# First norm by diagonal products, first stretch in a written order: one change to a hybrid streaming block on Trainium2

## The chip, the cores and the metric

The kernel runs on one core of a Trainium2 chip. A core has five engines that take their instructions from queues of their own and wait for each other by semaphores: TensorE (PE, matrix products, with PEld for its weight loads), VectorE (DVE), ScalarE (ACT), GpSimd (POOL) and SyncE (SP, which here only issues DMAs). The metric is the device time of one execution in microseconds (us), shown as a median of several runs. One execution of each kernel is also recorded by the hardware profiler; its span runs from the first instruction to the last.

## What is computed

The reference is one layer of an encoder over 1024 tokens of 1024 channels, all in float32. Cut to what matters here:

```python
def rmsnorm(x, g):
    y = x * lax.rsqrt(jnp.mean(x * x, axis=-1, keepdims=True) + EPS)
    return y * g

def swiglu(x, w_gate, w_up, w_down):
    return (jax.nn.silu(x @ w_gate) * (x @ w_up)) @ w_down

def reference(x, ...):
    x = x + 0.5 * swiglu(rmsnorm(x, ffn1_norm[l]), ffn1_w_gate[l], ffn1_w_up[l], ffn1_w_down[l])
    h = rmsnorm(x, mix_norm[l])
    ...
    x = x + 0.5 * swiglu(rmsnorm(x, ffn2_norm[l]), ffn2_w_gate[l], ffn2_w_up[l], ffn2_w_down[l])
    return rmsnorm(x, final_norm)
```

The inner width of each SwiGLU is 2816. The change concerns the first line: the first norm, and the first products that use it.

## The kernel before

**Precision.** Each float32 operand of a large product is split into a high part (a cast to fp32r on ScalarE) and a low part (the remainder, on VectorE or GpSimd). A product is three matmuls, high times high, high times low and low times high (`mm3`, all recorded at line 53). `split` makes both parts of a weight (L61, L62).

**Chunks.** The 2816 inner channels are 22 chunks of 128. Chunks 1 to 21 make gate and up together by a scheme of seven products instead of eight over 2 x 2 blocks (`gu`, 84 matmuls of 512 columns each). The normed, transposed x stands in four blocks: B11 (tokens of tiles 0 to 3, channels 0 to 511), B12 (tiles 4 to 7, channels 0 to 511), B21 (tiles 0 to 3, channels 512 to 1023), B22 (tiles 4 to 7, channels 512 to 1023). To these come four sums of blocks, T1 to T4, and sums of weight blocks, `s` (GpSimd, L191, in `load_gu`), whose split parts are named `gs`.

**The first stage.** Chunk 0 does not need the sums: `gu_plain` makes it by the eight plain products, in two halves of 256 columns per block, the first from token tiles 0, 1, 4 and 5, the second from 2, 3, 6 and 7: 96 matmuls a half. So TensorE has 64 transposes of 128 x 128, 192 matmuls of 256 columns and then chunk 1's 84 of 512 to do up to chunk 2. Chunk 1's products need T sums and split weight sums.

The norm comes ahead of the transposes. `normed` takes one tile of 128 tokens: square with a sum on ScalarE (L74), mean on VectorE (L76), the power on GpSimd (L70), and x times the factor times the norm row on VectorE (L82, a full row `grow` of 1024 values on each partition). The second four tiles have the same at L488 to L493. `blocks` then transposes by a product with the identity (L95) into a bank of PSUM, and ScalarE and VectorE take it out: the high and low parts of each block (`put`, L118 and L119; B12's at L141, L142) and the differences t3, t1, t2, t4 (L133, L137, L148, L150). `put_sums` makes the T sums from these, the T3 difference on GpSimd (L157).

**What sets the order.** The code is written loop by loop; a scheduler then reorders the built instructions of each engine by its own costs, and pools decide when a tile may be reused. Transfers of one queue (SP's and ScalarE's) are issued in the order in which the scheduler leaves them. Behind chunk 0, `weight_sums` makes sums of the down weights (loads L285, GpSimd L278, stores L293), for chunk pairs, and `hidden_sums` stores the hidden values (L296 to L307). PSUM has eight banks here, four under the tag "mm" for results, four under "ax".

## Time and profile before

| | |
|---|---|
| median of 3 runs | 1850.05 us (1845.16 to 1851.8) |
| the profiled execution's own time | 1841.2 us |
| its span | 1839.4 us |
| TensorE busy | 97% of the span |
| mean TensorE clock granted | 0.992 |

The profile gives the busy time of each engine, groups of instructions by line, and the timeline of each engine. In a timeline row stand the start and length in us, engine, line, operation, what it writes and reads, shape and count, and in brackets the idle time before it with what ended it. In a row of a stretch stand the busy times of PE, PEld, DVE, ACT and POOL, each with its count, then the granted clock of TensorE (1.00 is full), the mean busy share of the DMA engines and the GB/s moved. A wait of an engine that is not the bottleneck costs nothing by itself.

### The profile page before, as it was taken

The page shows a single profiled execution, that of the slowest core. Times are in us where ns is not written, and L with a number is a line of the kernel's source. Part 1 is how long each engine was busy: PE and PEld are TensorE (multiplying, and loading weights), DVE is VectorE, ACT ScalarE, POOL GpSimd, SP SyncE. Part 2 cuts the span into 40 slices and gives each one's busy share as a digit, 9 for nine tenths or more (in the row PEclk, how much of TensorE's full clock was granted, in tenths as well). Part 3 has the DMA queues.
Part 4 walks back from the last instruction along what each step waited for, and adds up shares of the span by engine and source line. Part 5 has one row for each costly group of instructions (what it writes and reads, how often), then busy time and mean ns, then how long its engine had stood idle before and what let it go on. Part 6 is the DMA issues. An engine that isn't in the chain of part 4 may idle for free.

```text
span 1839.4 us, 25484 instructions
## 1 busy us (share of the span) xinstructions
PE 1784.1 (97%) x9735; PEld 1524.8 (83%) x9735; DVE 1191.7 (65%) x1531; ACT 686.6 (37%) x1193; POOL 747.9 (41%) x583
## 2 busy tenths in 40 slices
PE   5999999999999999898999999999999999999997
PEld 4888888888788889797788989988888888878886
DVE  6867676665565575769655344587776766656546
ACT  6333332333343454432344533452333323243433
POOL 4667666565140012212132420366666665614001
PEclk9999999999999999999999999999999999999999
DMA  5353443544957445453432254334535445495744
GB/s 196 108 175 136 162 152 134 184 158 163 339 188 258 155 177 164 140 195 100 133 94 67 90 197 136 109 104 165 178 132 171 144 154 188 142 344 185 264 142 149
DMA packets 134441, 302.26 MB, mean 164 GB/s; under 512 B 27408, under 2 KB 42032, under 8 KB 134320
## 3 DMA queue, kind: packets, MB, share of 16 engines
q1 hardware_dynamic: 131824, 296.20, 46.9%
q10 hardware_dynamic: 2496, 4.44, 0.8%
q8 instruction: 76, 1.25, 0.3%
q14 instruction: 45, 0.37, 0.1%
HBM read 208.83 MB, written 91.77 MB: 163 GB/s over the span
## 4 chain that ended last, share of the span: by engine, by line
PE 78%; DVE 8%; DMA 5%; POOL 4%; issue 3%; ACT 2%; SPq 0%; POOLq 0%; DVEq 0%; ACTq 0%
PE mm L53 43%; PE ax L53 32%; POOL s L191 1%; POOL t L278 1%; DMA left<-hq 1%; DVE acc L873 1%; PE ax L95 1%; PE sd L53 1%; DMA graw<-in_f1gu_dram 1%; POOL s L278 1%; PE sc L53 1%; DVE T L119 0%; DVE unit L62 0%; DVE wk L62 0%; DVE E L797 0%
## 5 line engine op out<-in xcount | busy, mean ns | idle before, releaser
L53 PE MATMUL mm<-unit 128*128 128x512 f32 x1056 | 244.9, 392 | 4.2 <-ACT unit L61 2.2
L53 PEld LDWEIGHTS mm<-unit 128*128 128x128 f32 x1056 | 198.8, 189 | 47.4 <-ACT unit L61 3.3
L191 POOL TENSOR_TENSOR s<-graw 128x512 f32<-128x512 f32 x84 | 130.3, 1551 | 262.9 <-DMA graw<-in_f2gu_dram 116.0
L62 DVE TENSOR_TENSOR ga<-graw,ga 128x512 fp32r<-128x512 f32 x134 | 155.9, 1166 | 99.9 <-ACT ga L61 99.2
L61 ACT CAST gs<-s 128x512 fp32r<-128x512 f32 x168 | 104.5, 622 | 301.8 <-PE mm L53 151.0
L62 DVE TENSOR_TENSOR unit<-left,unit 128x1024 fp32r<-128x1024 f32 x84 | 101.9, 1215 | 133.0 <-ACT unit L61 132.3
L53 PE MATMUL ax<-T,gs 128*128 128x512 f32 x792 | 183.1, 389 | 0.0
L53 PE MATMUL ax<-unit 128*128 128x512 f32 x792 | 180.5, 389 | 0.0
L53 PEld LDWEIGHTS ax<-T,gs 128*128 128x128 f32 x792 | 148.7, 188 | 30.8
L53 PEld LDWEIGHTS ax<-unit 128*128 128x128 f32 x792 | 148.7, 188 | 30.8
L62 DVE TENSOR_TENSOR gs<-s,gs 128x512 fp32r<-128x512 f32 x168 | 172.7, 1030 | 2.3
L53 PE MATMUL mm<-B,ga 128*128 128x512 f32 (+1 forms) x864 | 166.8, 347 | 3.3 <-ACT B L118 1.9
L61 ACT CAST unit<-left 128x1024 fp32r<-128x1024 f32 x84 | 82.5, 982 | 230.2 <-PE ax L53 100.5
L53 PE MATMUL mm<-T,gs 128*128 128x512 f32 x720 | 166.5, 389 | 0.0
L53 PEld LDWEIGHTS mm<-B,ga 128*128 128x128 f32 x864 | 139.5, 194 | 23.4 <-ACT B L118 2.5
L53 PEld LDWEIGHTS mm<-T,gs 128*128 128x128 f32 x720 | 135.2, 188 | 28.0
L70 POOL TENSOR_TENSOR rs<-rs,half 128x1 f32<-128x1 f32 (+1 forms) x29 | 19.2, 662 | 334.5 <-DVE rs L76 334.4
L53 PE MATMUL mm<-actT,wk 128*128 128x512 f32 x576 | 150.4, 403 | 0.0
L53 PE MATMUL ax<-B,ga 128*128 128x512 f32 x528 | 127.2, 390 | 1.4 <-DVE ga L62 1.4
L53 PE MATMUL mm<-wk,actT 128*128 128x256 f32 x960 | 123.5, 285 | 2.7 <-DVE wk L62 2.7
L53 PEld LDWEIGHTS mm<-wk,actT 128*128 128x128 f32 x960 | 117.4, 190 | 3.4 <-DVE wk L62 3.0
L53 PEld LDWEIGHTS mm<-actT,wk 128*128 128x128 f32 x576 | 103.6, 188 | 18.8
(239 smaller groups left out, 3046.0 us busy)
## 6 DMA issues: line engine op xcount, KB each, us to landing
left<-hq SPq DMA_DIRECT2D x70, 512.0 KB, 5.0
graw<-in_f1gu_dram SPq DMA_DIRECT2D x44, 512.0 KB, 5.4
wq<-t SPq DMA_DIRECT2D x44, 512.0 KB, 2.8
hq<-s SPq DMA_DIRECT2D x44, 512.0 KB, 3.1
graw<-in_f2gu_dram SPq DMA_DIRECT2D x44, 512.0 KB, 4.7
right<-wq SPq DMA_DIRECT2D x40, 512.0 KB, 4.8
wd<-in_f1wd_dram SPq DMA_DIRECT2D x22, 512.0 KB, 6.6
hq<-sg SPq DMA_DIRECT2D x22, 512.0 KB, 3.7
```

Source lines behind the costliest of these rows:

```text
L53: nc.tensor.matmul(*args, **kw)
L61: nc.scalar.copy(h, src)
L62: nc.vector.tensor_tensor(l, src, h, op=ALU.subtract)
L70: nc.gpsimd.tensor_tensor(o, i, half[:, :w], op=ALU.pow)
L95: nc.tensor.transpose(ps[:, i * P:(i + 1) * P], blk(i), ident)
L191: nc.gpsimd.tensor_tensor(f, u, v, op=op)
L278: nc.gpsimd.tensor_tensor(o, u, v, op=op)
L873: nc.vector.scalar_tensor_tensor(acc, pad[:, j:j + 512], cw[:, blk, j:j + 1], acc, op0=ALU.mult, op1=ALU.add)
```

## The change

The first norm is no longer made on x. ScalarE squares a tile, GpSimd adds the constant and takes the power, and ScalarE multiplies the identity by the four factors of a group of tiles: a 128 x 128 diagonal per tile (`factors`, L545 and L550 of the changed kernel). TensorE multiplies x's columns by that diagonal, which transposes and scales at once (`turn` in `scaled_blocks`), where before it transposed: 64 float32 products of 128 x 128 in place of 64 transposes. The norm's gain, which now lies along partitions, is a factor in each evacuation: `put` and `t3` on ScalarE (L166, L188: a multiplication), `less` on VectorE (L163: multiply and subtract). It comes as a small load of 128 x 8 values (`f1g`) in place of the full row.

A column of `scaled_blocks` is one bank: 128 channels by 512 tokens, u (the tiles of B11 or B21) and v (those of B12 or B22). For columns 0 to 3, ScalarE makes B11's high part, t3 and B12's high part and VectorE B11's low part, B12's low part and t1; for columns 4 to 7, ScalarE makes the high parts of B21 and B22 and VectorE both low parts, t2 and t4.

Further: x is loaded in the order 0, 1, 4, 5, then 2, 3, 6, 7; 20 products of the identity with itself stand ahead of all others on TensorE, and are used by nothing; the table of Silu is loaded at the start; `gu_plain` yields in groups of 12 products and goes through the channels one after the other in this stage; each T sum's parts are made for 256 columns at once (`scaled_sum`); the order on TensorE, VectorE, ScalarE and GpSimd up to the last T part and weight split of chunk 1 is the one in which the code is written (`manual_schedule`); the down-weight sums of the first pair go from chunk 1 to chunk 2; the loads of norm rows keep their place in the written order. Four working tiles of the second half come from the pools of x (three) and of raw weights (`t4`, under the tag "graw"). The second SwiGLU computes as before, with the changed function called through `together`.

```diff
-        nc.scalar.dma_start(g, a[name].to_broadcast([P, D]))
+        tc.keep_in_program_order(nc.scalar.dma_start(g, a[name].to_broadcast([P, D])))
...
-        def put(self, n, i, src, eng):
+        def __init__(self, qp, bp):
+            self.qp, self.bp, self.B, self.f = qp, bp, {}, {}
+        def block(self, n):
             if n not in self.B:
                 if n in ("T1", "T3", "B21"):
                     self.B[n] = act_tile(self.bp, "cmb", n, bufs=3)
                 else:
                     self.B[n] = act_tile(name=n)
-            t = self.B[n][:, :, :, i * P:i * P + P]
+            return self.B[n]
+        def put(self, n, i, src, eng):
+            t = self.block(n)[:, :, :, i * P:i * P + P]
             nc.scalar.copy(t[:, 0], src)
             eng.tensor_tensor(t[:, 1], src, t[:, 0], op=ALU.subtract)
 
...
+        def scaled_blocks(self, i, pp, xts, dg, g, f, b12, ahead):
+            sl = slice(i * 256, i * 256 + 256)
+            t3, t1, t2, t4 = self.f[i] = f
+            def less(o, src, c, v):
+                nc.vector.scalar_tensor_tensor(o, src, g[:, c:c + 1], v, op0=ALU.mult, op1=ALU.subtract)
+            def put(h, l, src, c):
+                nc.scalar.mul(h, src, g[:, c:c + 1])
+                less(l, src, c, h)
+            banks = []
+            def turn(k):
+                cs = range(len(banks), len(banks) + k)
+                banks.extend(bank(*pp) for _ in cs)
+                for n, x in enumerate(xts):
+                    for c in cs:
+                        mm(banks[c][:, n * P:n * P + P], x[:, c * P:c * P + P], dg[:, n * P:n * P + P], start=True, stop=True)
+            turn(ahead)
+            for c in range(8):
+                if c == len(banks):
+                    turn(1)
+                u, v = banks[c][:, :256], banks[c][:, 256:]
+                k = c % 4
+                if c < 4:
+                    b = self.block("B11")
+                    put(b[:, 0, k, sl], b[:, 1, k, sl], u, c)
+                    nc.scalar.mul(t3[:, k], u, g[:, c:c + 1])
+                    b = b12[k // 2]
+                    put(b[:, 0, k % 2], b[:, 1, k % 2], v, c)
+                    less(t1[:, k], v, c, t3[:, k])
+                else:
+                    b = self.block("B21")
+                    put(b[:, 0, k, sl], b[:, 1, k, sl], u, c)
+                    b = self.block("B22")
+                    put(b[:, 0, k, sl], b[:, 1, k, sl], v, c)
+                    less(t2[:, k], v, c, t1[:, k])
+                    less(t4[:, k], u, c, t2[:, k])
+                yield
+        def scaled_diff(self, i):
+            t3, _, t2, _ = self.f[i]
+            nc.gpsimd.tensor_tensor(t3, t2, t3, op=ALU.subtract)
+        def scaled_sum(self, i, n, eng):
+            src = self.f[i][{"T1": 1, "T2": 2, "T3": 0, "T4": 3}[n]]
+            t = self.block(n)[:, :, :, i * 256:i * 256 + 256]
+            nc.scalar.copy(t[:, 0], src)
+            eng.tensor_tensor(t[:, 1], src, t[:, 0], op=ALU.subtract)
...
-        def gu_plain(sl, b12):
+        def gu_plain(sl, b12, by_k=False):
             g = gu_s[0]
             w = sl.stop - sl.start
             gates, ups = ([bank(*A)[:, :w] for _ in range(2)] for _ in range(2))
             xs = {n: partial(lambda n, s, k, sl: B[n][:, s, k, sl], n) for n in ("B11", "B21", "B22")}
             xs["B12"] = lambda s, k, sl: b12[k // 2][:, s, k % 2]
-            for i, x in ((0, "B11"), (1, "B12"), (0, "B21"), (1, "B22")):
-                first = x[1] == "1"
-                for p, wt in ((gates[i], g["B11" if first else "a12"]), (ups[i], g["a21" if first else "a22"])):
-                    products(p, wt, xs[x], sl, first, not first)
+            todo = [(first, k, i, j) for first in (True, False) for k in range(4) for i in range(2) for j in range(2)]
+            if not by_k:
+                todo.sort(key=lambda s: (not s[0], s[2], s[3], s[1]))
+            for n, (first, k, i, j) in enumerate(todo):
+                x = xs[(("B21", "B22"), ("B11", "B12"))[first][i]]
+                p, wt = (gates[i], ups[i])[j], g[(("a12", "a22"), ("B11", "a21"))[first][j]]
+                mm3(p, wt[:, 0, k], wt[:, 1, k], x(0, k, sl), x(1, k, sl), first and k == 0, not first and k == 3, skip_group_check=True)
+                if n % 4 == 3:
+                    yield
 ...
         start(SimpleNamespace(load_gu=load_gu, gu=gu, gu_plain=gu_plain, gtile=gtile, A=A, X=X))
         xts = {}
         for c in range(1, NCH):
-            together(load_gu(c))
-            if c % 2:
+            if c not in gu_s:
+                together(load_gu(c))
+            if c % 2 and c > late:
                 weight_sums(c // 2)
-            else:
+            elif c % 2 == 0:
+                if c // 2 * 2 == late + 1:
+                    weight_sums(0)
                 hidden_sums(c // 2 - 1)
...
-    xs = load_x(xdram, (0, 4))
-    g = grow("ffn1_norm")
-    xs.update(load_x(xdram, (1, 5)))
+    nc.scalar.dma_start(g1, a["f1g"])
+    xs = load_x(xdram, (0, 1, 4, 5))
...
-            def xi(i):
-                return xs[i], xs[i + 4]
-            uv = [cb.sums() for _ in range(2)]
-            for j in range(2):
-                for i in range(2):
-                    normed(xi(i)[j], g, xi(i)[j], uv[i][j])
+            order = ((0, 1, 4, 5), (2, 3, 6, 7))
+            def factors(ts):
+                ms, rs = (sm.tile([P, 4], F32, tag=n, name=n) for n in ("ssk", "rk"))
+                dg = rp.tile([P, 544], F32, tag="sf", name="dg", bufs=4)[:, :512]
+                for n, t in enumerate(ts):
+                    junk = f.gtile(F32, "junk").rearrange("p s n -> p (s n)")
+                    m, r = ms[:, n:n + 1], rs[:, n:n + 1]
+                    nc.scalar.activation(junk, xs[t], AF.Square, scale=D ** -0.5, accum_out=m)
+                    nc.gpsimd.tensor_scalar(r, m, EPS, None, op0=ALU.add)
+                    rpow(r, r, 1)
+                yield dg
+                for n in range(4):
+                    nc.scalar.mul(dg[:, n * P:n * P + P], ident, rs[:, n:n + 1])
+                yield
...
+            def four(ts):
+                return [t.rearrange("p a (b n) -> p (a b) n", b=2) for t in ts]
+            E = mybir.EngineType
-            together(*(cb.put_sums(i, ("T2", "T1", "T3", "T4"), (V, G, V, G)) for i in range(4)))
+            with tc.manual_schedule(engines={E.PE, E.DVE, E.Activation, E.Pool}):
+                warm = bank(*f.X)
+                for _ in range(20):
+                    mm(warm[:, :P], ident, ident, start=True, stop=True)
+                nc.scalar.activation(half[:, 7:8], half[:, 6:7], AF.Silu)
+                facs = [factors(t) for t in order]
+                dg = next(facs[0])
+                together(facs[0])
+                together(f.load_gu(0, True))
+                xs.update(load_x(xdram, order[1]))
+                b = b12()
+                bl = cb.scaled_blocks(0, f.X, [xs[t] for t in order[0]], dg, g1, four(cb.sums() + cb.sums()), b, 4)
+                pr = f.gu_plain(slice(0, 256), b, True)
+                together(islice(bl, 4))
+                for k in range(4):
+                    next(pr)
+                    next(bl)
+                    if k == 1:
+                        dg = next(facs[1])
+                together(facs[1])
+                cb.scaled_diff(0)
+                together(pr)
+                t4 = rp.tile([P, 1088], F32, tag="graw", name="t4", bufs=4)[:, :D].rearrange("p (a n) -> p a n", a=2)
+                fs = four([xp.tile([P, 2, 512], F32, tag="x", name="f") for _ in range(3)] + [t4])
+                b = b12()
+                bl = cb.scaled_blocks(1, f.X, [xs[t] for t in order[1]], dg, g1, fs, b, 1)
+                pr = f.gu_plain(slice(256, 512), b, True)
+                for n, eng in (("T1", G), ("T2", V), ("T3", V), ("T4", G)):
+                    next(bl)
+                    cb.scaled_sum(0, n, eng)
+                weights = f.load_gu(1)
+                for k in range(4):
+                    next(pr)
+                    next(bl)
+                    if k == 0:
+                        next(weights)
+                    elif k == 1:
+                        cb.scaled_sum(1, "T1", G)
+                cb.scaled_sum(1, "T2", V)
+                next(weights)
+                cb.scaled_diff(1)
+                next(weights)
+                together(pr)
+                next(weights)
+                cb.scaled_sum(1, "T3", V)
+                next(weights)
+                next(weights)
+                cb.scaled_sum(1, "T4", G)
+                together(weights)
...
-        ffn(cb, a["f1gu"], a["f1wd"], ps, rp, gp, qp, bp, start1, load_xts, to_mid, {2: [after]}, z0)
+        ffn(cb, a["f1gu"], a["f1wd"], ps, rp, gp, qp, bp, start1, load_xts, to_mid, {2: [after]}, z0, 1)
...
-        x=x, ffn1_norm=ffn1_norm, mix_norm=mix_norm, ffn2_norm=ffn2_norm, final_norm=final_norm.reshape(1, D),
+        x=x, f1g=ffn1_norm.reshape(KC, P).T, mix_norm=mix_norm, ffn2_norm=ffn2_norm, final_norm=final_norm.reshape(1, D),
```

On TensorE the program before starts as follows (from its first row; `ident` is the identity, `ga` the split weights of chunk 0, B_172 a part of B11, B_164 and B_165 of B12):

```order
L95 MATMUL ax<-ident,x 128x128 x16
L53 MATMUL mm<-B_172,ga_150 128x256
L53 MATMUL mm<-B_172,ga_153 128x256
L95 MATMUL ax<-ident,x 128x128 x8
L53 MATMUL mm<-B_172,ga_150 128x256 x11
L53 MATMUL mm<-B_172,ga_153 128x256 x11
L53 MATMUL mm<-B_164,ga_150 128x256 x6
```

and now as follows (`dg` are the diagonals, B_214 is a part of B11, B_188 of B12):

```order
L53 MATMUL ax<-ident 128x128 x20
L53 MATMUL ax<-dg,x 128x128 x16
L53 MATMUL mm<-B_214,ga_168 128x256 x3
L53 MATMUL mm<-B_214,ga_171 128x256 x3
L53 MATMUL mm<-B_188,ga_168 128x256 x3
L53 MATMUL mm<-B_188,ga_171 128x256 x3
L53 MATMUL ax<-dg,x 128x128 x4
```

The plain products come in twelves, one twelve to a column, with the four diagonal products of a later column behind each. Behind chunk 1 the rows of TensorE are the same in both programs.

ScalarE took the first blocks out of PSUM before in this order (with what each row waits for; `f` are t1 to t4):

```order
L133 COPY f<-ax 128x512 [waits PE_49,Activation_49]
L118 CAST B_172<-ax 128x4x128
L118 CAST B_208<-ax 128x4x128 [waits PE_49] x2
L141 CAST B_164<-ax 128x2x128 [waits DVE_49] x2
L118 CAST T_551<-f 128x4x128 x2
```

and takes columns 4 to 7 of the first half now in this one (B_260 is a part of B21, B_263 of B22, `ba` holds the gain; L545 are the squares of the second four tiles):

```order
L166 ACTIVATE B_260<-ax,ba 128x256 [waits PE_49]
L166 ACTIVATE B_263<-ax,ba 128x256 [waits DVE_49]
L545 ACTIVATE junk,ssk<-x 128x1024 [waits DMAHW0_49,Activation_49]
L545 ACTIVATE junk,ssk<-x 128x1024 [waits DMAHW1_49,Activation_49]
L545 ACTIVATE junk,ssk<-x 128x1024 [waits DMAHW2_49,PE_49,Activation_49]
L545 ACTIVATE junk,ssk<-x 128x1024 [waits DMAHW3_49,Activation_49]
L166 ACTIVATE B_260<-ax,ba 128x256
L166 ACTIVATE B_263<-ax,ba 128x256 [waits DVE_49]
```

The squares of the second four tiles have moved between two columns, and the second read of a bank by ScalarE waits for VectorE's read of it. VectorE's rows of the first three columns are now (L163 is `less`):

```order
L163 SCALAR_TENSOR_TENSOR B_214<-ax,ba,B_214 128x256 [waits DMAHW2_49,Activation_49]
L163 SCALAR_TENSOR_TENSOR B_188<-ax,ba,B_188 128x256 [waits Activation_49]
L163 SCALAR_TENSOR_TENSOR f<-ax,ba,f 128x256
L163 SCALAR_TENSOR_TENSOR B_214<-ax,ba,B_214 128x256 [waits Activation_49]
L163 SCALAR_TENSOR_TENSOR B_188<-ax,ba,B_188 128x256 [waits Activation_49]
L163 SCALAR_TENSOR_TENSOR f<-ax,ba,f 128x256
```

where each L163 that waits for ScalarE subtracts the high part which ScalarE has just made.

SP's queue held from the start (`graw` are raw weights, `wd` down weights, `wq` and `hq` stores):

```order
L451 DMA x<-in_x_dram 128x1024 x4
L185 DMA graw<-in_f1gu_dram 128x1024 x2
L451 DMA x<-in_x_dram 128x1024 x4
L185 DMA graw<-in_f1gu_dram 128x1024 x4
L285 DMA wd<-in_f1wd_dram 128x1024 x2
L293 DMA wq_112<-t_619 128x2x512
```

and holds now:

```order
L520 DMA x<-in_x_dram 128x1024 x4
L244 DMA graw<-in_f1gu_dram 128x1024 x2
L520 DMA x<-in_x_dram 128x1024 x4
L244 DMA graw<-in_f1gu_dram 128x1024 x3
L364 DMA hq_105<-sg 128x512
L244 DMA graw<-in_f1gu_dram 128x1024 x3
L349 DMA wd<-in_f1wd_dram 128x1024 x2
```

A chunk has two `graw` loads. Chunk 2's are the third and fourth behind the second x loads; the second of them now stands behind the store of chunk 0's hidden values (L364), and the down weights have moved behind chunk 3's loads.

More of the change, by code (lines that the diff above doesn't have):

```diff
@@ L163, in together, with ffn @@
             pass
-    def ffn(cb, wgu, wd, ps, rp, gp, qp, bp, start, load_xts, emit, before={}, fill=None):
+    def ffn(cb, wgu, wd, ps, rp, gp, qp, bp, start, load_xts, emit, before={}, fill=None, late=0):
         A, X = (ps[0], "mm"), (ps[1], "ax")
@@ L444, in block_kernel @@
     sp = {n: dr.tile([8, P, 512], F32, tag="sp" + n, name="sp" + n) for n in "zvm"}
-    ba = cp.tile([P, 16, 8], F32, tag="ba", name="ba")[:, :8]
+    ba = cp.tile([P, 16, 8], F32, tag="ba", name="ba")
+    g1 = ba[:, 8]
+    ba = ba[:, :8]
     def load_x(src, ts):
@@ L475, in b12 @@
             def b12():
                 return [f.gtile(F32R, "B12").rearrange("p s (k n) -> p s k n", k=2) for _ in range(2)]
-            weights = f.load_gu(0, True)
-            next(weights)
-            xs.update(load_x(xdram, (2, 6, 3, 7)))
-            b = b12()
-            parts = [cb.blocks(i, f.X, xi(i), uv[i], b) for i in range(2)]
-            together(*parts, n=2)
-            together(*parts, weights)
-            rest = xi(2) + xi(3)
-            ms = sm.tile([P, 4], F32, tag="ssk", name="ms4")
@@ L594, in w_out @@
                 yield
-        cb = Combos(g2, qp, bp)
+        cb = Combos(qp, bp)
         pp = (ps[1], "ax")
```

20 lines of the change are left out of this document (3 added, 17 removed).

## The prediction

> **What bounds the kernel now.** I read the page (two rows), then the stretches of ten microseconds (PE, PEld, DVE, ACT and POOL busy, granted clock, DMA share, GB/s), then TensorE's timeline (start, length, instruction, count, idle time before and what ended it).
>
> ```profile
> span 1839.4 us, 25484 instructions
> PE 1784.1 (97%) x9735; PEld 1524.8 (83%) x9735; DVE 1191.7 (65%) x1531; ACT 686.6 (37%) x1193; POOL 747.9 (41%) x583
> ...
> 0.00:10.00 10.00, 0.64 (x3) 0.65 (x4) 1.50 (x3) 3.49 (x6) 0.74 (x5) 1.00 0.78 290
> 10.00:20.00 10.00, 6.95 (x31) 5.45 (x30) 8.33 (x13) 6.42 (x14) 1.62 (x3) 1.00 0.99 398
> 20.00:30.00 10.00, 9.41 (x78) 9.06 (x77) 9.54 (x14) 9.94 (x21) 7.74 (x6) 1.00 0.15 54
> 30.00:40.00 10.00, 4.86 (x35) 4.48 (x34) 6.50 (x5) 4.47 (x10) 7.24 (x6) 0.84 0.15 52
> 40.00:50.00 10.00, 7.30 (x32) 6.23 (x31) 9.55 (x17) 7.02 (x15) 4.42 (x4) 0.50 0.37 130
> 50.00:60.00 10.00, 10.00 (x83) 10.00 (x83) 10.00 (x11) 5.72 (x12) 8.67 (x6) 0.98 0.12 45
> 60.00:70.00 10.00, 8.58 (x41) 6.90 (x40) 10.00 (x11) 2.62 (x5) 7.62 (x6) 1.00 0.43 157
> 70.00:80.00 10.00, 10.00 (x45) 8.28 (x45) 8.00 (x10) 3.37 (x6) 5.70 (x4) 1.00 0.27 88
> ...
> 16.26 0.78 PE L53 MATMUL mm<-B,ga 128*128 128x256 f32 x2
> ...
> 17.30 1.97 PE L95 MATMUL ax<-ident,x 128*128 128x128 f32 x8 [0.26 <-DVE B L119]
> ...
> 22.84 1.04 PE L95 MATMUL ax<-ident,x 128*128 128x128 f32 x8
> ...
> 62.67 2.57 PE L53 MATMUL ax<-B,ga 128*128 128x512 f32 x10 [1.42 <-DVE ga L62]
> ...
> 81.40 2.88 PE L53 MATMUL mm<-B,ga 128*128 128x512 f32 x12
> ```
>
> TensorE is busy 97% of the span. In the stretch rows its busy time up to 70 us adds to 47.7, so 22 us of its idle time lie in the first stage, and the clocks 0.84, 0.50 and 0.98 of the three stretches from 30 on mean 3.2 + 10 + 0.4 = 13.6 us at 0.50. The start was slow too, though its rows say 1.00: eight transposes took 1.97 us at 17.30 and 1.04 at 22.84, that is steps of 0.21 and 0.11. From 62.67 TensorE runs without a gap; chunk 2 starts at **81.40**. In the built program TensorE's rows from there to the end are the same. So the change is worth the shift of that one start.
>
> **The change part by part.** The rows nearest to what is new on TensorE and at the start, from the timeline, the list of transfers (the last number is us from issue to landing) and the groups (busy us, mean ns, idle before):
>
> ```profile
> 755.52 0.66 PE L844 MATMUL ax<-ident,kst 128*128 128x128 f32 x4 [2.25 <-ACT kst L875]
> 756.01 1.06 PE L53 MATMUL sd<-kst 128*128 128x128 f32 x8
> ...
> 50.78 9.40 PE L53 MATMUL mm<-B,ga 128*128 128x256 f32 x77
> ...
> 0.72 0.40 ACTq L454 DMA_DIRECT2D ident<-in_cst_dram  x1
> ...
> ident<-in_cst_dram ACTq DMA_DIRECT2D x1, 64.0 KB, 4.0
> ...
> 8.94 1.06 ACT L74 ACTIVATE f<-x 128x1024 f32<-128x1024 f32 x1 [3.23 <-DMA x<-in_x_dram]
> ...
> L657 POOL TENSOR_SCALAR rs<-rs 128x1 f32<-128x1 f32 x1 | 0.2, 190 | 0.1
> ...
> 10.36 0.55 POOL L70 TENSOR_TENSOR rs<-rs,half 128x1 f32<-128x1 f32 x1 [3.82 <-DVE rs L76]
> ```
>
> *Products.* Four F32 products of kst stand in the program for these eight records: each is two passes of 0.11, so 0.22 us, where a transpose is one (0.11; four took 0.66, with the last one's tail). A diagonal product therefore costs two transposes: 64 x 0.22 = 14.1 us at full clock against 7.0. The 192 products of 256 columns stay, 0.12 each (9.40 / 77).
>
> *Warm-up.* 20 identity products are 40 passes. The identity lands at 0.72 + 4.0 = 4.7. All at half clock they end at 4.7 + 40 x 0.213 = 13.2, all at full at 9.1. In the trace products became dense at 16.26; those at 17.30 still step at 0.21, those at 22.84 at 0.11, so the clock rose 3 to 6.6 us after. I take 5 us at half (23 passes) and 17 passes at 0.11: **11.6**.
>
> *Factors.* The third tile issued was there at 8.94, so the fourth about 1.3 later (512 KB at the 398 GB/s of 10:20), 10.2; without the 512 KB of the norm row, 8.9. Then the square 1.06, POOL 0.19 + 0.55 and the last diagonal 0.37 (priced below): 11.1, hidden by the warm-up; were that gone, 11.1 would set the start. Sixteen diagonal products then end at 11.6 + 3.6 = **15.2**. The norm rows' loads that now keep program order are issued somewhat later; the last is used 600 us after its issue:
>
> ```profile
> L66 ACTq DMA_DIRECT2D grow<-in_final_norm_dram x1: 335/335/335, 1197.0 to 1197.0; - x1
> ...
> L82 DVE SCALAR_TENSOR_TENSOR o<-x,rs,grow x7: 1283/1285/1287, 1800.9 to 1831.0; 128x1024 f32<-128x1024 f32 x7
> ```
>
> *Evacuation.* This decides. Each new operation reads 128x256 from a bank with a factor per partition:
>
> ```profile
> L1027 ACT ACTIVATE oh<-sq,ex 128x128 f32<-128x128 f32 x32 | 11.8, 368 | 16.4 <-PE sq L53 16.0
> ...
> L896 ACT ACTIVATE kst<-ax 128x128 f32<-128x128 f32 x32 | 8.4, 276 | 2.6 <-PE ax L844 2.6
> ...
> L243 ACT ACTIVATE sg<-mm 128x256 f32<-128x256 f32 x8 | 3.0, 383 | 5.6 <-PE mm L53 5.6
> ...
> L908 DVE SCALAR_TENSOR_TENSOR aT<-sc,br,E 128x128 f32<-128x128 f32 x16 | 4.5, 343 | 0.0
> ...
> L1025 DVE TENSOR_TENSOR u<-u,sc 128x128 f32<-128x128 f32 x32 | 9.1, 286 | 17.3 <-PE sc L53 16.1 <-ACT u L994 1.1
> ...
> L142 DVE TENSOR_TENSOR B<-ax,B 128x256 fp32r<-128x256 f32 x16 | 6.5, 417 | 0.9 <-ACT B L141 0.7
> ...
> 42.60 0.37 ACT L141 CAST B<-ax 128x256 fp32r<-128x256 f32 x1 [1.58 <-DVE f L137]
> 42.87 0.62 ACT L118 CAST T<-f 128x512 fp32r<-128x512 f32 x1
> ...
> 48.85 0.38 ACT L141 CAST B<-ax 128x256 fp32r<-128x256 f32 x1
> ...
> 49.26 0.42 DVE L142 TENSOR_TENSOR B<-ax,B 128x256 fp32r<-128x256 f32 x1
> ```
>
> At 128 columns the factor adds 0.09 on ScalarE (368 against 276) and 0.06 on VectorE (343 against 286). I put these on 0.383 and 0.417: **0.48** and **0.47** per operation; the ends are no surcharge (0.38, 0.41) and twice it (0.57, 0.53). On one engine the next starts 0.10 early (42.60 to 42.87); a handover costs 0.03 (48.85 + 0.38 to 49.26). The order shows that ScalarE and VectorE never read one bank together: ScalarE's second read waits for VectorE's first, as the cast at 42.60 waited 1.58 us for a VectorE read of its bank.
>
> The Trainium skill, PSUM — Partial Sum Buffer, section Terms, says that two engines may not access one bank at once, reads included. By it the waits cannot be dropped; the trace agrees with the 1.58 us at 42.60. Were there no such rule, three operations of each engine would lie beside each other, 1.2 us a column, and the sum would be that of the first rival.
>
> Columns 0 to 3 of the first half, each: VectorE 0.47, ScalarE 0.37 + 0.48, VectorE 0.39 + 0.39, three handovers: 2.2; four make 8.8, to 24.0. TensorE needs 12 x 0.12 + 4 x 0.22 = 2.3 beside each. Columns 4 to 7: VectorE 0.47, ScalarE 0.48, VectorE 0.39 + 0.47 + 0.39: 2.3 each, 9.2, to 33.2. Between columns 5 and 6 ScalarE makes four squares, 4 x 1.06; VectorE and then TensorE wait about 3.3 of it (the last 0.9 of column 5 lies beside the first): 36.5.
>
> The second half starts with a bank of four diagonal products (0.9): 37.4. Its columns 0 to 3 carry the first half's T casts and two T remainders:
>
> ```profile
> L61 ACT CAST unit<-left 128x1024 fp32r<-128x1024 f32 x70 | 73.7, 1053 | 189.9 <-PE ax L53 79.9 <-PE mm L53 67.9 <-DMA left<-hq 31.0
> ...
> L62 DVE TENSOR_TENSOR unit<-left,unit 128x1024 fp32r<-128x1024 f32 x70 | 90.5, 1294 | 107.1 <-ACT unit L61 106.3 <-DMA hq<-sg 0.6
> ...
> L62 DVE TENSOR_TENSOR ga<-graw,ga 128x512 fp32r<-128x512 f32 x134 | 155.9, 1166 | 99.9 <-ACT ga L61 99.2
> ...
> L191 POOL TENSOR_TENSOR s<-graw 128x512 f32<-128x512 f32 x84 | 130.3, 1551 | 262.9 <-DMA graw<-in_f2gu_dram 116.0 <-DMA graw<-in_f1gu_dram 104.8 <-DVE up L274 13.2
> ```
>
> ScalarE's own work then ends last: 0.48, 0.37, 0.48, a cast of 0.95 (1.05 less the overlap) and VectorE's 0.47 make 2.8; with a T remainder of 1.3 on VectorE ahead of the next column, whose ScalarE reads it delays, 3.6. So 2.8 + 2.8 + 3.6 + 3.6 = 12.8, to 50.2. Columns 4 to 7 again 9.2, and one weight remainder of 1.17 on VectorE: 60.6. Then the last T cast 0.95, its remainder 1.3 and two weight remainders of 1.17, with handovers 4.7: 65.3. POOL's two sums for them (1.55 each) were made before 61. By then TensorE has done 16 of chunk 1's 84 products; 68 x 0.227 (2.72 per twelve) = 15.4. Chunk 2 starts at **80.7**, against 81.40: **0.7 us earlier**. The profiled execution takes 1841.2 for a span of 1839.4, so it becomes 1840.5. The median of the runs shown, 1850.05, stands 8.9 above it; on it the forecast is **1849.3**.
>
> What costs nothing: POOL's weight sums and SP's two loads and two stores for them go from chunk 1 to chunk 2, where POOL has 4.3 us idle in ten (70:80). The table load for Silu goes under the wait for the first tile.
>
> The ends: 16 columns with two to three operations in series on each engine move by 0.25 to 0.35 each if the surcharge is none or double: 5 us either way. The warm-up moves 2.5 earlier (but then the factors hold it at 11.1) or 1.6 later. The tail of 4.7, means over mixed lengths, has 1.0 either way. Together 6.5 earlier to 7.6 later.
>
> **Rivals.**
> 1. *The evacuation hides and TensorE's work bounds.* 11.6 + 14.1 + 192 x 0.12 + 84 x 0.227 = 67.8, 13.6 earlier, **1836.5**. It needs column turns below 2.3 in the second half too, where ScalarE alone has 2.3 with its cast. Against it: the waits in the order.
> 2. *Slower: the clock stays at half.* TensorE idles 3 to 4 us at the four squares, as it did before its clock fell (30:40 has 4.86 busy). At half a column costs TensorE 12 x 0.21 + 4 x 0.43 = 4.2, not 2.3. Left from 33 on: 120 products and 32 diagonal ones, 21.5 at full, 43 at half; evacuation needs 32, so TensorE has some 10 us to lose, which is 20 us at half clock; each microsecond beyond costs half. At half to the end of the plain products: 33 + 43 + 19 = 95, 13.6 later, **1863.7**. It decides from 20 us on; for the 13.6 us of before I put +1 at most. Before, dense products ended it, and products that take 4.2 against turns of 2.3 are dense.
> 3. *Chunk 2's weights late.* Their second load reuses the tile of the last T sum. Its cast stands eight ScalarE operations behind the last T cast named above, at about 68.5, and POOL reads it 2 x 1.55 longer. Then the load lands, POOL makes two sums, and a cast and a remainder follow:
>
> ```profile
> graw<-in_f1gu_dram SPq DMA_DIRECT2D x44, 512.0 KB, 5.4
> ```
>
> 68.5 + 3.1 + 5.4 + 3.1 + 0.6 + 1.2 = 81.9, against a need at 80.7 + 2.7 = 83.4. Three microseconds more in that chain would cost two: **1851**.
> 4. *The change does not do what it says*: the clock does not rise in the warm-up. Then it ends at 13.2 and the sixteen products take 6.8: 4.7 later, **1854**.
>
> The Trainium skill, TensorE: Matmul & The Clock Gate, Part 1, says the clock halves after an idle window of about 3.4 us and returns after a busy one. By it rival 2 lasts one or two windows and the sum moves by about 1 us; the 13.6 us here fit four such windows, too thinly filled to return.
>
> **How the numbers follow.** Forecast 0.68, rival 1 0.12, rival 2 0.08, rival 3 0.07, rival 4 0.05. The median of three runs itself moves (1845.16 to 1851.8). The range takes the bounds of the unknown costs and some of that: 1840 to 1858. About 0.5% is what a measurement of this kernel can tell from no change, 9.25 us here; only rivals 1 and 2 cross it, with a little from the tails: faster 0.14, same 0.77, slower 0.09.
>
> **What would show it.** Chunk 2's first 512-column product near 80.7; 40 warm-up passes from 4.7 to 11.6; L163 and L166 at 0.47 and 0.48 taking turns, with waits for each other in nearly every column; a gap of 3 to 4 us on TensorE before column 6; T and gs remainders ending chunk 1's last wait. Column turns below 2 us, a clock at 0.50 through the second half, or a new wait behind 81 would prove me wrong.

## The result

The changed kernel takes 1860.08 us in the median (1857.44 to 1862.42), the kernel before 1849.12 beside it: a ratio of **1.0053**, 95% interval [1.0028, 1.0078], slower by 11 us. The profiled executions lie further apart, 1859.77 against 1841.2 us, because that of before was one of its fastest: over all runs here it took 1838.8 to 1863.8. The spread of the kernel before goes with the mean granted clock of each run: about 1842 us at 0.992, 1846 at 0.990, 1851 at 0.987 and 1862 to 1864 at 0.980 to 0.982. Both profiled executions had 0.992, so their difference is not one of the mean clock. What follows finds the difference of the two profiles, 18.6 us, and then asks how much of it the median holds.

The page's head and TensorE's timeline of the changed kernel (start, length, instruction, count, idle time before and what ended it):

```profile
span 1858.0 us, 25729 instructions
PE 1803.1 (97%) x9839; PEld 1536.5 (83%) x9839; DVE 1155.2 (62%) x1538; ACT 688.9 (37%) x1209; POOL 748.9 (40%) x588
...
4.82 6.29 PE L53 MATMUL ax<-ident 128*128 128x128 f32 x40 [4.82 <-DMA ident<-in_cst_dram]
10.95 3.74 PE L53 MATMUL ax<-dg,x 128*128 128x128 f32 x32
14.58 2.77 PE L53 MATMUL mm<-B,ga 128*128 128x256 f32 x12
...
31.14 5.05 PE L53 MATMUL mm<-B,ga 128*128 128x256 f32 x24 [3.05 <-ACT B L166]
36.03 3.74 PE L53 MATMUL ax<-dg,x 128*128 128x128 f32 x32
...
65.65 9.17 PE L53 MATMUL ax<-T,gs 128*128 128x512 f32 x32 [0.95 <-DVE gs L62]
...
82.81 2.88 PE L53 MATMUL mm<-B,ga 128*128 128x512 f32 x12
...
233.37 3.02 PE L53 MATMUL ax<-B,gs 128*128 128x512 f32 x12 [1.30 <-DVE pe L328]
...
472.46 4.53 PE L53 MATMUL ax<-T,ga 128*128 128x512 f32 x12 [4.91 <-DVE up L330]
478.10 0.50 PE L53 MATMUL mm<-unit 128*128 128x512 f32 x1 [1.10 <-ACT unit L61]
...
762.71 4.50 PE L53 MATMUL mm<-wk,actT 128*128 128x256 f32 x24 [2.87 <-ACT pad L981]
...
772.58 1.05 PE L956 MATMUL ax<-ident,kst 128*128 128x128 f32 x4 [3.53 <-ACT kst L987]
```

The same timeline of the kernel before has no wait between 66 us and this row, the first product with the hidden values (`unit`):

```profile
464.33 0.50 PE L53 MATMUL mm<-unit 128*128 128x512 f32 x1 [1.97 <-ACT unit L61]
```

Row against row, the changed kernel is **1.4 us** late at chunk 2 (82.81 against 81.40), **13.8** at the first product of hidden values (478.10 against 464.33), **17.1** at the transposes of kst (772.58 against 755.52), and 18.6 at the end. So the first stage, which the whole prediction was about, came out 1.4 us to the bad, and 17 us were lost behind it, where TensorE does the same in the same order. The 1.4 us are not clear of chance: later profiles with the same first stage start chunk 2 at 83.27 (e11, that of before) and 82.68 (e6, the change's).

**The first place** lies between chunk 2 and the hidden products. The waits there are small and of one kind (six, 0.25 to 1.30 us, as at 233.37), and one large at 472.46. Each small one waits for VectorE to empty a bank (`pe`), and VectorE is late because the split of the chunk's weights stands ahead of it. That split waits for ScalarE's cast, the cast for GpSimd's sums, and these for the load. Here are GpSimd and VectorE ahead of the wait at 233.37:

```profile
228.27 1.28 POOL L250 TENSOR_TENSOR s<-graw 128x512 f32<-128x512 f32 x1 [8.24 <-DMA graw<-in_f1gu_dram]
...
231.60 1.12 DVE L62 TENSOR_TENSOR gs<-s,gs 128x512 fp32r<-128x512 f32 x1 [6.95 <-ACT gs L61]
232.64 0.68 DVE L328 TENSOR_TENSOR pe<-ax,pe 128x512 f32<-128x512 f32 x1
```

SP's queue shows when the loads came. Here are the four loads of chunks 1 and 2 (in the changed kernel chunk 2's second with chunk 3's two), the first store of down-weight sums (`wq`) for chunk 3, and from TensorE chunk 3's start, in the kernel before and then in the changed one:

```profile
8.94 20.62 SPq L185 DMA_DIRECT2D graw<-in_f1gu_dram  x4
...
104.57 3.77 SPq L293 DMA_DIRECT2D wq<-t  x2
...
100.44 2.88 PE L53 MATMUL ax<-B,ga 128*128 128x512 f32 x12
```

```profile
72.56 1.48 SPq L244 DMA_DIRECT2D graw<-in_f1gu_dram  x3
...
118.95 3.79 SPq L357 DMA_DIRECT2D wq<-t  x2
...
102.49 2.88 PE L53 MATMUL ax<-B,ga 128*128 128x512 f32 x12
```

I call the distance of the last two (store behind product) the **lag** of the weight loop (loads, GpSimd's sums, splits, stores): 4.1 us before, 16.5 now. Chunk 2's second load is issued at 72.56, with chunk 3's right behind; before, chunk 2's loads were issued by 29.6.

The large wait is the same lateness at the end of the stage. VectorE's and ScalarE's timelines there, changed kernel:

```profile
469.51 1.04 ACT L61 CAST unit<-left 128x1024 fp32r<-128x1024 f32 x1 [14.92 <-DMA left<-hq]
...
470.58 1.23 DVE L62 TENSOR_TENSOR unit<-left,unit 128x1024 fp32r<-128x1024 f32 x1 [10.45 <-ACT unit L61]
471.73 0.68 DVE L330 TENSOR_TENSOR up<-ax,pe 128x512 f32<-128x512 f32 x1
```

The load of the hidden values stands in SP's queue behind the late stores, its split stands in VectorE's queue ahead of the evacuation of chunk 21's last bank (L330), and TensorE waits 4.91 us for that bank, then runs at a lower clock (0.73 in 470 to 475). Counted by the starts of TensorE's rows, with what it needs to get going again behind each wait, the small waits make 6.5 of the 12.4 us lost in this stage and the end of the stage 5.9.

**The second place** is near 750 us, in the decay matrices, which no line of the change touches. GpSimd's timeline of before, then of the changed kernel, with VectorE's rows beside it:

```profile
735.64 1.53 POOL L799 TENSOR_TENSOR E<-csa,grb 128x512 f32<-128x512 f32 x1 [3.79 <-DMA grb<-grd]
```

```profile
750.34 9.03 POOL L911 TENSOR_TENSOR E<-csa,grb 128x512 f32<-128x512 f32 x1 [4.04 <-DMA grb<-grd]
...
750.98 0.68 DVE L914 TENSOR_TENSOR E<-E,csa 128x512 f32<-128x512 f32 x1
...
757.01 1.21 DVE L62 TENSOR_TENSOR wk<-raw,wk 128x1024 fp32r<-128x1024 f32 x1
```

One operation of the same shape takes 9.03 us instead of 1.53. It is ready at 750.34, while VectorE runs one operation after the other without a gap until 758.22, and it ends 1.15 us after VectorE does. ScalarE stands still for what GpSimd makes, and its copy (`pad`), for which TensorE waits at 762.71, comes behind that:

```profile
760.52 0.63 ACT L913 ACTIVATE E<-E 128x512 f32<-128x512 f32 x1 [5.83 <-POOL E L912]
...
762.09 0.56 ACT L981 COPY pad<-mm 128x512 f32<-128x512 f32 x1
```

### The profile page after: what moved, and what is told of

Same layout as the page of the kernel before. It is cut to its first block, busy times and chain, and to the rows that moved or that the text cites. A ratio compares the mean times of both kernels' runs of the same rounds, so it can differ in the third digit from the quotient of the medians.

```text
span 1858.0 us, 25729 instructions
## 1 busy us (share of the span) xinstructions
PE 1803.1 (97%) x9839; PEld 1536.5 (83%) x9839; DVE 1155.2 (62%) x1538; ACT 688.9 (37%) x1209; POOL 748.9 (40%) x588
## 4 chain that ended last, share of the span: by engine, by line
PE 75%; DVE 8%; DMA 6%; POOL 5%; ACT 3%; issue 3%; SPq 0%; POOLq 0%; DVEq 0%; ACTq 0%
PE mm L53 42%; PE ax L53 30%; DMA graw<-in_f1gu_dram 3%; POOL s L250 2%; POOL s L342 1%; DMA left<-hq 1%; DVE acc L985 1%; PE sd L53 1%; PE ax L95 1%; DVE ga L62 1%; PE sc L53 1%; DVE B L163 1%; DVE gs L62 1%; POOL E L911 0%; DVE o L82 0%
## 5 line engine op out<-in xcount | busy, mean ns | idle before, releaser
L62 DVE TENSOR_TENSOR gs<-s,gs 128x512 fp32r<-128x512 f32 x168 | 186.6, 1113 | 103.8 <-ACT gs L61 102.6
L250 POOL TENSOR_TENSOR s<-graw 128x512 f32<-128x512 f32 x84 | 121.8, 1450 | 271.2 <-DMA graw<-in_f1gu_dram 130.8
L62 DVE TENSOR_TENSOR ga<-graw,ga 128x512 fp32r<-128x512 f32 x134 | 144.3, 1080 | 70.7 <-ACT ga L61 70.2
L53 PE MATMUL mm<-B,ga 128*128 128x512 f32 (+1 forms) x864 | 170.8, 347 | 6.4 <-ACT B L166 3.1
L70 POOL TENSOR_TENSOR rs<-rs,half 128x1 f32<-128x1 f32 x24 | 16.0, 665 | 323.5 <-DVE rs L76 323.4
```

Of the source, the lines that this page charges most:

```text
L53: nc.tensor.matmul(*args, **kw)
L62: nc.vector.tensor_tensor(l, src, h, op=ALU.subtract)
L70: nc.gpsimd.tensor_tensor(o, i, half[:, :w], op=ALU.pow)
L250: nc.gpsimd.tensor_tensor(f, u, v, op=op)
```

## The experiments

Theories, as they stood before the first runs: **L**, the lag carries the loss behind chunk 2; **S**, chunk 2's second load alone does; **C**, the loss comes from clock windows that come anyhow. The kernel before ran beside each group, at medians of 1848.9 us (e1 to e4), 1845.4 (e5 to e12) and 1846.2 (e13, e14), so groups are compared by their ratios to it; the changed kernel's is 1.0053. Each run moves a working tile or some instructions, leaves out the warm-up or repeats one sum; none changes what is computed. Each was profiled once.

**e1 to e4: the two edits that delay the loop, taken back, and one of them alone.**

```diff
-                t4 = rp.tile([P, 1088], F32, tag="graw", name="t4", bufs=4)[:, :D].rearrange("p (a n) -> p a n", a=2)
+                t4 = qp.tile([P, 2, 512], F32, tag="post", name="t4", bufs=4)        # e1, e3
-        ffn(cb, ..., {2: [after]}, z0, 1)
+        ffn(cb, ..., {2: [after]}, z0, 0)                                            # e2, e3
```

e4 is the kernel before with the new `late=1` alone.

> The changed kernel with one edit: the working tile t4 comes from the pool of the first half's working tiles instead of a raw-weight tile, so that chunk 2's second weight load no longer waits for it. Theory L (lead): from chunk 2 on loads, GpSimd sums, splits and stores form a loop that takes about 38.9 us a pair of chunks against 38.1 on TensorE; only the lead with which it starts protects TensorE, and the change took 14 us of it, part by the tile and part by the down-weight sums. Then this gives back some 4 us of lead: second pair's wq store near 115 instead of 119, time about 1855. Rival S (single load): the tile alone took the lead: store near 105, time about 1846. Rival C (clock): the loss behind chunk 2 is idle windows that come anyhow: time stays at 1860.

> The changed kernel with one edit: the first pair's down-weight sums are again issued with chunk 1. Theory L: lead is back by the 7 us of GpSimd work that leave chunk 2, though two of the loads now stand ahead of weights in SP's queue: store of the second pair between 105 and 112, time 1848 to 1856. Rival S: chunk 2's second load is as late as before, 1860. Rival C: 1860.

> The changed kernel with both edits. Theory L: the lead is that of the kernel before (store of the second pair near 105), no stall over 0.2 us of TensorE between chunk 2 and chunk 21, and time 1844 to 1851. Rival S: the same as with the tile alone. Rival C: 1860.

> The kernel before with one part of the change alone: the first pair's down-weight sums go from chunk 1 to chunk 2. Theory L: the lead shrinks by about 7 to 14 us; stalls before gs products as in the changed kernel, 0.3 to 1.9 us a pair, and a wait of some us at the first product of the hidden values; time 1852 to 1860. Rival S: 1849, as the kernel before. Rival C: 1849.

Measured: e1 1853.94 us, 1.0016 [0.9993, 1.0039]; e2 1853.19, 1.0026 [1.0003, 1.0049]; e3 1852.69, 1.0016 [0.9994, 1.0039]; e4 1845.33, 0.9973 [0.9945, 1.0002]. Each edit alone takes away 0.27 to 0.37%, 5 to 7 of the 11 us, both together no more. The intervals overlap that of the changed kernel, but the stage itself is clear: none of the three has a wait of 0.2 us or more from 90 us to the hidden products, and C falls. S falls too, since e2 leaves the load late (76.23). But L as I had it was wrong in two points. The sums moved alone (e4) do no harm, the lag is 8.5 us. And the loop does not run at 38.9 us a pair by itself: in e1, lag 11.8, it kept TensorE's pace to the end of the stage. The drift of before, 4.1 to 11.2, was a loop falling back to where it rests. In e1 to e3, chunk 2 itself came 4 to 5 us later than in the changed kernel (86.68 in e1). The causes differ. In e1, 1.0 us of the 3.9 is a longer warm-up (7.25 against 6.29), which the edit does not touch; in e2, TensorE waits 4.90 us at 57.82 for a weight split whose load stands behind one of down weights in SP's queue. In e1 and e3 GpSimd now makes sums of chunk 2 ahead of the last T remainder (rows of e1), but how much that costs is not shown:

```profile
72.48 2.26 POOL L250 TENSOR_TENSOR s<-graw 128x512 f32<-128x512 f32 x1
74.71 2.84 POOL L210 TENSOR_TENSOR T<-t,T 128x1024 fp32r<-128x1024 f32 x1
```

**e5 to e8: the tile in the kernel before, the slow GpSimd operation, the squares, the warm-up.**

```diff
+            t24 = rp.tile([P, 1088], F32, tag="graw", name="t24", bufs=4)[:, :D].rearrange("p (s n) -> p s n", s=2)
+                uv3 = cb.sums(xp) if i == 2 else [xp.tile([P, 2, 512], F32, tag="x", name="f"), t24]   # e5, on e4
-            eng = nc.vector if hf else nc.gpsimd
+            eng = nc.vector                                                                            # e6
-                    if k == 1:
-                        dg = next(facs[1])
+                    if k == 0:
+                        dg2 = next(facs[1])
+                    next(facs[1])                                                                      # e7: factors yields once a tile
-                for _ in range(20):
-                    mm(warm[:, :P], ident, ident, start=True, stop=True)                               # e8
```

> The kernel of the run e4 (before, down-weight sums with chunk 2), and besides one working tile of its second half in a raw-weight tile, as the change has it, so that chunk 2's second load waits for the last T sum. Theory L: the lead falls (second pair's wq store more than 12 us behind chunk 3's first product; 8.5 in e4, 16.7 in the changed kernel, 11.8 in e1), stalls of 0.3 us and more before gs products come back, and the wait of some 5 us at the last ga products of the stage; time 1850 to 1858. Rival F (only a written first stage makes the loop late, the tile does not): as e4, 1845.

> The changed kernel with one edit far behind the first stage: the two operations of the decay matrices that GpSimd makes (9.0 us for one of them in the changed kernel's profile near 750 us, 1.5 in the kernel before's) go to VectorE. Theory P: that one operation waits for eleven VectorE operations in a row, and about 4.7 us of the loss are the wait of TensorE behind it: no wait of 2.9 us for the pad copy, shift against the kernel before 13 to 15 us behind it instead of 18 to 19, time 1854 to 1857. Rival: the wait comes from the clock or the loads, time 1860.

> The changed kernel with the second four squares one behind each of columns 4 to 7 instead of all behind column 5. Theory Q: the idle 3.05 us of TensorE and the two slow microseconds of clock behind it go, chunk 2 starts near 78 instead of 82.8; the lead of the weight loop, counted from TensorE, is then smaller still, since its loads wait for the T sums: the stalls behind chunk 2 eat part, time 1855 to 1859. Rival: VectorE and ScalarE take turns anyway, the four squares only spread the same wait: chunk 2 at 82, time 1860.

> The changed kernel without the 20 identity products, which nothing uses. Theory W: the sixteen diagonal products start at 10.5 to 11 as before, but at half clock, 6.8 us for 3.7, and the clock rises some 4 us later: chunk 2 starts 3 to 5 us later, time 1863 to 1866 unless the loop behind, already late, hides it (then 1860). Rival N: the clock is full from the start and the warm-up only delays: chunk 2 not later, time 1858 to 1860.

Measured: e5 1841.37 us, 0.999 [0.9971, 1.0009]; e6 1849.05, 1.0009 [0.9989, 1.0029]; e7 1859.06, 1.0065 [1.0044, 1.0086]; e8 1854.43, 1.0051 [1.0035, 1.0066]. e5 went as rival F had it: a tile in that place does not make the loop late where the first stage is the old one (lag 9.9, no stall). The last of its first four weight loads went out by 49.9 us, where the changed kernel's came at 72.56. e7 closed the idle time before column 6 and won 1.5 us at chunk 2 (81.28), not the 4 to 5 expected: its warm-up happened to take 1.1 us longer (7.39 against 6.29), and after 26.09 the four columns run without a gap, only slower.

```profile
26.09 7.98 PE L53 MATMUL mm<-B,ga 128*128 128x256 f32 x48
```

e8 is the surprise. Without the warm-up the sixteen diagonal products take 5.45 us instead of 3.74, as if a part of them ran at half clock, and end 1 us later. At the T products e8 is 1.4 us behind (67.08 against 65.65), but these run at full clock (32 in 7.56 us against 9.17), and chunk 2 starts at 82.67, no later than with the warm-up. The time by its ratio is the changed kernel's. But behind chunk 2 its profile goes another way, after the last of these rows:

```profile
10.20 5.45 PE L53 MATMUL ax<-dg,x 128*128 128x128 f32 x32 [10.20 <-ACT dg L550]
...
67.08 7.56 PE L53 MATMUL ax<-T,gs 128*128 128x512 f32 x32 [0.96 <-DVE gs L62]
...
98.69 4.60 PE L53 MATMUL mm<-B,gs 128*128 128x512 f32 x12 [2.27 <-DVE pe L328]
```

TensorE waits once, by 2.27 us at chunk 2, and not once more up to the hidden products, which come 7.6 us earlier than in the changed kernel (470.46): the lag, which counts from TensorE, is then 14.7 and falls pair by pair. e6's own lag was 15.9 and stayed. This gave L its present form, a bound between 14.7 and 15.9.

**e9 to e12: the fastest combination, a dose of lag, and the GpSimd operation in three settings.** e9 is e5 with e6's edit, e11 the kernel before with it, e12 e1 with it. e10 is e4 with

```diff
-            sub(t34[:, 1], b21, t12[:, 1])
+            for _ in range(8 if late and q == 1 else 1):
+                sub(t34[:, 1], b21, t12[:, 1])
```

> The kernel of e5 with the decay matrices wholly on VectorE as in e6. By theory P the operation of 9.1 us near 732 us in e5's profile goes, and with it the wait of 2.7 us for the pad copy and the slow clock behind it. Chunk 2 starts at 75.7 as in e5, 5.7 us before the kernel before. Time 1836 to 1840 in nearly all runs, without e5's second cluster at 1848 to 1852; faster than the kernel before by 0.3 to 0.5%. Rival: e5's two clusters come from something else, and the median stays at 1841 with runs at 1850.

> The kernel of e4 with one of GpSimd's sums for the second pair made eight times over (the same result; 7 more operations of 1.74, 12.2 us, at chunk 3). Lag is the time of a pair's wq store behind the first product of its odd chunk: 8.5 in e4, 16.7 in the changed kernel. Theory L, as refined (a lag below some 15 shrinks to 11, a longer one stays and holds TensorE back by 0.3 to 1.9 us a pair): lag of the third pair above 16, stalls before gs products in several pairs, the 5 us wait at the last ga products of the stage, and 1852 to 1858. Rival R (a loop that is late catches up in a pair or two): at most one stall at chunk 3 or 4, no wait at the end of the stage, 1845 to 1849.

> The kernel before with the decay matrices wholly on VectorE. Theory P: the kernel before has the 9 us operation in some runs and not in others (its times go from 1841 to 1851), so without it the median falls to 1840 to 1843 and the spread narrows. Rival: its profile shows 1.5 us for the operation, so nothing is gained; 8 more operations of 0.68 on VectorE cost up to 5 us, 1845 to 1850.

> The changed kernel with t4 in a tile of its own (e1) and the decay matrices on VectorE (e6): both losses taken away behind a first stage that is the change's. What is left by theory L and P is the first stage (chunk 2 at 86.7, 5.3 late): 1845 to 1849. Rival: the gains of e1 (6) and e6 (11) are one and the same, then 1849 to 1853.

Measured: **e9 1835.22 us** (1833.76 to 1836.81), 0.995 [0.9934, 0.9967], faster than both kernels; e11 1839.02, 0.9967 [0.9944, 0.9991]; e12 1844.41, 1.0002 [0.9987, 1.0016]; e10 1846.78, 1.0023 [0.9998, 1.0047]. With both losses taken away behind the changed first stage (e12) it takes the time of the kernel before. That is 0.51% less than the changed kernel, against 0.37 for e1 and 0.44 for e6, so by the times the two do not add up in full, though each figure is uncertain by some 0.2; in its profile neither loss is left (383.0 us from chunk 2 to the hidden products, no wait for the pad copy). Beside e11, which has the same edit and the old first stage, e12 is still 0.35% slower; chunk 2 (85.2 against 83.3) has 1.9 us of that. In the profiles e12 is 6.2 us behind at the transposes of kst and 10.3 at the end, but its profiled execution was its slowest (1851.37), so this does not divide the 0.35%. e10 decides nothing, its dose left a lag of only 13.9. In its profiled run TensorE also ran at a granted clock of about 0.50 from 900 to 920 us; that is not explained.

**e13 and e14: larger doses**, ten and thirteen in place of eight.

> As e10, with the sum made ten times over (9 more operations, 16 us) for chunk 3. e10's dose left a lag of 13.9 at the third pair, below the bound of some 15. Theory L: lag of the third pair near 17, and then it stays at 16 to 18, with stalls before gs products in several pairs (sum over 1 us from 150 to 440 us) and a wait near 5 us at the last ga products of the stage; 6 to 10 us slower than e4 at the start of the hidden products. Rival R: one stall near chunk 4 or 5, then the lag falls pair by pair to 11 or 12 as in e8, no wait at the end of the stage.

> As e13, with 12 more operations (21 us). Theory L: a stall of some us near chunk 4 or 5 brings the lag to 16 to 18, where it stays, with the same small stalls and the wait at the end of the stage. Rival R: a stall of 3 to 8 us near chunk 4 or 5, no other, lag back to 12 by the end of the stage.

Measured: e13 1852.84 us, 1.0036 [1.0013, 1.0060]; e14 1855.03, 1.0059 [1.0036, 1.0083], against 0.9973 of e4. TensorE's waits in e13:

```profile
342.10 3.01 PE L53 MATMUL ax<-B,gs 128*128 128x512 f32 x12 [0.79 <-DVE pe L264]
380.96 3.01 PE L53 MATMUL ax<-B,gs 128*128 128x512 f32 x12 [0.39 <-DVE pe L264]
466.37 5.49 PE L53 MATMUL ax<-T,ga 128*128 128x512 f32 x12 [6.09 <-DVE up L266]
```

A delay on GpSimd at chunk 3 (ten operations of 16.38 us in all for one of 1.74), and nothing else against e4, brings the whole picture into a kernel with the old first stage: small waits of the same kind, over 200 us later, and the large one at the end of the stage. e14 has the same, behind a first wait of 2.41 us at 132.98. R expected the lag to fall; it rose. This table is worked out from the timelines of SP and TensorE of each profile (us); the last column is the time from chunk 2 to the first product of hidden values.

| kernel | chunk 2 | lag, chunk 3 | chunk 5 | chunk 11 | chunk 19 | to hidden |
|---|---|---|---|---|---|---|
| before | 81.4 | 4.1 | 5.9 | 8.9 | 11.2 | 382.9 |
| e4 | 78.7 | 8.5 | 9.2 | 9.3 | 11.2 | 382.7 |
| e5 | 75.7 | 9.9 | 11.2 | 11.2 | 11.8 | 383.6 |
| e1 | 86.7 | 11.8 | 11.3 | 11.2 | 12.1 | 382.9 |
| e10 | 79.6 | 8.5 | 13.9 | 13.9 | 12.3 | 383.0 |
| e8 | 82.7 | 14.7 | 14.7 | 12.9 | 11.7 | 387.8 |
| e6 | 82.7 | 15.9 | 16.4 | 16.7 | 17.9 | 391.2 |
| e7 | 81.3 | 16.3 | 17.0 | 17.8 | 17.8 | 394.1 |
| after | 82.8 | 16.5 | 17.0 | 18.1 | 17.5 | 395.3 |
| e13 | 79.4 | 8.5 | 16.3 | 17.7 | 17.5 | 392.6 |
| e14 | 78.7 | 8.5 | 16.1 | 17.0 | 17.6 | 396.1 |

Up to 14.7 the lag goes to 11 or 12 and the stage takes 383 us (388 with e8's one wait and the clock behind it); e2, e3, e9, e11 and e12, with lags of 5.4 to 12.8 at chunk 3, go the same way. From 15.9 the lag goes to 17 or 18 and stays, at a cost of 8 to 13 us. By the doses alone, which do not hold TensorE up first as e8's wait does, the bound lies between 13.9 and 16.1. The changed kernel and e6 are the same up to the decay matrices, so the 4 us between their stages (395.3, 391.2) is what single profiles scatter. What holds it at 17 is not shown. In the queues, GpSimd makes the hidden sums behind the next chunk's weight sums, and SP loads weights behind the store of those hidden sums, so a late load delays the next one; why this closes at 16 was not tried.

**The GpSimd operation.** In sixteen profiles it takes 1.39 to 1.59 us in four (before, e2, e4, e7), 9.03 to 9.35 in eight (after, e1, e3, e5, e8, e10, e13, e14), and is on VectorE in four. From the first product of hidden values to the transposes of kst these take 289.6 to 291.2, 292.2 to 295.3, and 283.4 to 287.6 us. So the long form costs some 3.4 us by the means, and the wait for the pad copy, 2.86 to 2.88 us, is there in all eight and in no other. e6's edit gains more than that, since the order around it changed too: before's own waits of 2.75 and 2.25 there are gone as well in e11. So the edit does not price the long form: it gains 0.33% in the kernel before, whose one profile has the short form, and 0.44% in the changed kernel. What decides between the forms is not shown. In both, GpSimd is ready in the same place of VectorE's order, 0.23 to 0.56 us behind the start of the same pair of operations, in e4 (short) and in e3 (long) 0.25 us behind:

```profile
730.73 2.40 DVE L799 TENSOR_TENSOR E<-grb,gc 128x512 f32<-128x512 f32 x2
730.98 1.59 POOL L801 TENSOR_TENSOR E<-csa,grb 128x512 f32<-128x512 f32 x1 [3.74 <-ACT E L805]
...
740.72 1.28 DVE L909 TENSOR_TENSOR E<-grb,gc 128x512 f32<-128x512 f32 x2
740.97 9.35 POOL L911 TENSOR_TENSOR E<-csa,grb 128x512 f32<-128x512 f32 x1 [3.73 <-ACT E L915]
```

Whether the kernel before falls into the long form in part of its executions wasn't seen: only one was profiled, and its spread goes with the clock. e11 still had two runs above 1844.

## Why the prediction was wrong

- **The step that failed** is the one that ended "What bounds the kernel now": that TensorE's rows behind chunk 2 are the same, so that the change is worth the shift of that one start. The rows are the same, and in the profiles 17 of 18.6 us are lost between them: 12.4 at the waits that the late loop makes up to the hidden products, 3.3 at the decay matrices, 1.5 behind. The step takes an engine that runs without a gap as one that can't be made to wait. Its reserve was a queue of loads and sums that ran ahead of need, and the change spent 12 us of it.
- **Rival 3 had the place and the time, not the size.** It put chunk 2's second load at 71.6 (measured 72.56) and asked only whether chunk 2 gets its weights by 83.4. It does, nearly: the wait is 0.34. But chunk 3's loads and the down weights stand behind that load in the queue, and the lateness is handed on for nineteen chunks. I priced it at 2 us more; the stage lost 12.4 in the profile, and e1 to e3 gave back 5 to 7 of the median.
- **"What costs nothing: POOL's weight sums and SP's two loads and two stores"** was right of the move alone (e4), wrong beside the late load: e2 gained 0.27%, 5 us, by taking it back. Idle time of GpSimd per ten microseconds did not say whether it comes before or after the load that is waited for.
- **The first stage was right nearly to the end.** Warm-up to 10.95 (11.6 forecast), sixteen products to 14.6 (15.2), a gap of 3.05 at the squares (3.3), columns done at 60.8 (60.6), last splits at 65.65 (65.3). The warm-up's end is partly luck: in seven profiles with the same warm-up it took 6.17 to 7.39 us. So is the last figure: the last T remainder ahead of it took 2.49 us (1.3 forecast) and the two weight remainders 1.7 each (1.17), but TensorE went on behind the first of these. Evacuation came out nearly as taken, 0.47 on ScalarE (0.48) and 0.48 on VectorE (0.47):

```profile
L166 ACT ACTIVATE B<-ax,ba 128x256 fp32r<-128x256 f32 x32 | 14.4, 472 | 11.3 <-DVE B L163 9.5 <-PE ax L53 1.8
...
L163 DVE SCALAR_TENSOR_TENSOR B<-ax,ba,B 128x256 fp32r<-128x256 f32 x32 | 15.4, 482 | 16.9 <-ACT B L166 16.9
```

  Chunk 2 was forecast at 80.7 and came at 82.81; of these 2.1 us, 0.35 are the later start and 1.75 the 32 products at 65.65, which took 9.17 us at a clock of 0.57 (66 to 70), 9.00 to the next row, where I had 7.25 at full clock. The Trainium skill, TensorE: Matmul & The Clock Gate, Part 1, puts the loss of clock at an idle window of some 3.4 us; here TensorE was busy for 2.04 of the 4 us ahead (62 to 66), with waits of about 1 us, so the clock fell without an idle stretch of that length.
- **The warm-up** did raise the clock as said, but in the one profile without it (e8) it was worth 1.4 us at the T products, little more than the 1.2 us by which its own length varies, and nothing at chunk 2. Rival 4's price of 4.7 was too high: without any warm-up the sixteen products took 5.45 us, not the 6.8 of half clock throughout, 1.7 more than with it.
- **No rival had the GpSimd operation.** No edit but e6's touches those lines, and both forms occur with the same lines (short in e4, long in e10). The Trainium skill, SBUF — State Buffer, section SBUF: two separate sides, says that GpSimd and a VectorE operation with two inputs in SBUF lock a pair of ports for the whole instruction, and that whoever starts first gets it. The trace agrees that one of the two stands still, but where the operation was long GpSimd did not get its turn after one instruction: it stood through about a dozen of them.

## What to carry over

An engine that never waits has its reserve in some queue. Before counting a change behind it as free, find how far the loads and sums run ahead of it, which instruction starts them, and whether a late one is handed on from round to round; a small late start can then cost at every round, or, under a bound, nothing. A wait far behind an edit that touches only the start can be a coincidence of two engines, so compare the long instructions of both profiles by name, not only the waits.

## Unexpected on the hardware

- A GpSimd tensor_tensor of 128x512 took 9.03 to 9.35 us in eight profiles and 1.39 to 1.59 in four. In the changed kernel it was ready while VectorE ran operations on SBUF back to back, and ended 1.15 us after the last of them. In the kernel before it was ready in the same place, at 735.64, 0.30 us behind the start of a VectorE operation, and went on at once; there VectorE's pair of operations took longer instead (two in 2.38 us, against two in 1.28):

```profile
735.34 2.38 DVE L797 TENSOR_TENSOR E<-grb,gc 128x512 f32<-128x512 f32 x2
...
740.90 1.28 DVE L797 TENSOR_TENSOR E<-grb,gc 128x512 f32<-128x512 f32 x2
```

- The weight loop had two states that hold, with lags near 11 and near 17.5 us, and in e8 one wait of 2.27 us of TensorE went ahead of the way from 14.7 back to 11.7: with it TensorE reached the hidden products 7.6 us earlier than the changed kernel did without it.
